# Output projection as seven block products, first gates applied earlier, second head's loads issued earlier

## The chip, the cores and the metric

The kernel runs on one core of one Trainium2 chip. The metric is device time in microseconds (us) of one execution, as the median of several runs. The engines are named as in the profile: PE (matrix products and transposes), PEld (its weight loads), DVE, ACT and POOL (elementwise work), SP (which issues most DMA transfers; its queue is written SPq, and ACT's ACTq).

## The reference, cut to what matters

One block works on x of 1024 tokens by 1024 columns in fp32:

```python
h = rms_norm(x, norm1_g[l])
z = h @ w_in[l]
glu_in, q, k, v, gate_logits = jnp.split(z, SPLITS, axis=-1)
a = a_val * jax.nn.sigmoid(a_gate)           # from glu_in
a = silu(rms_norm(causal_depthwise_conv(a, conv_w[l], conv_b[l]), conv_norm_g[l]))
y_a = a @ w_conv_out[l]
...                                          # 16 heads, three dilated windows, mixed into o
y_b = o @ w_attn_out[l]
g = jax.nn.sigmoid(gate_logits + gate_b[l])
g_a, g_b = jnp.split(g, 2, axis=-1)
x = x + (g_a * y_a + g_b * y_b) @ w_out[l]
h = rms_norm(x, norm2_g[l])
u = causal_depthwise_conv(h @ w_up[l], ffn_conv_w[l], ffn_conv_b[l])
x = x + (silu(u_gate) * u_val) @ w_down[l]
```

The change touches three things: where `sigmoid(...)` of the first half of the gates and its product with `y_a` are computed, the product with `w_out` (1024 x 1024 x 1024), and the order of some loads near the start of the attention.

## The kernel before, in words

Every fp32 operand of a product is split in two parts of the type fp32r: `hi`, a copy by ACT, and `lo`, the rest, a subtraction on DVE (`split`, L106 and L107). A product then is three matmuls, hi by hi, hi by lo and lo by hi, summed in PSUM. A full matmul takes a 128 x 128 stationary operand and 512 columns.

The program runs in stages, one after the other on PE: the products of the convolution branch and of most gates, in pairs of 128-row blocks (a stage called the pairs here); queries and keys; values; the attention; the merge; the output projection; the up and down products of the feed-forward part. Some products are already made in seven instead of eight block products (the pairs, the values, the up products). Between the heads' own matmuls the attention runs a filler (`side_steps`): the last gate products (`gate`, L138 to L140 by `gemm_half`) and the product of the convolution branch with `w_conv_out` (`conv_out`), a few steps in each of the eight slots of a head.

**Gates.** The sixteen gate blocks go unsigmoided to DRAM (`dgate`): those of the pairs from `begun` and the code around it, the last four from `gate` during the attention. `conv_out` stores y_a (`dya`).

**Merge** (`gate_pair`, `merge`). For each of eight column blocks `c` and two token halves, two gates and y_a are loaded, both gates go through the sigmoid (L1502, L1503), y_a is multiplied by the first (L1504). PE makes `yb` (24 matmuls), DVE multiplies it by the second gate (L1524), adds (L1525), and the sum is split into `mT` (L1527 on ACT, L1528 on DVE).

**Output projection** (`wo_piece`, `wo_tile`, `wo_add`). For each column half j and each of eight token tiles, `gemm_tok` runs 24 matmuls (L155 to L157) into one of the four banks of psB. The weights of a half come in four pieces of 512 KB (`raw_wo`), each split by L1535 and L1536. DVE adds the row of x (L1619), the sum goes to DRAM (`dx2`), and ACT squares it for the norm (L1621). In the second half the first half of the row is loaded back, `wo_scaled` (L1630) multiplies the row by its rstd (a power on POOL, L131) and by g2, and `transpose_raw` (L1598) turns it on PE for the up products. Beside it, `forms_ahead` prepares combinations of up weights and stores them (`dform`).

**What sets the order.** In the attention ACT, DVE, PE and POOL run in the order in which the code is written (`manual_schedule`), as ACT, DVE and PE do in the last part of the output projection and the up products. Elsewhere a planner orders the instructions. SP's order is always the planner's; `issue_after` keeps an instruction from being put ahead of another in it. SP takes its transfers one by one, in its order: one that waits for data or for a buffer holds all behind it. Each DMA of SP also waits for the one eight earlier on its semaphore.

**Attention, first heads.** Head h's queries, keys and mask are loaded by `head(h)`, its values by `values(h)`. `tiles[h + 1] = head(h + 1)` stands at place 1 of head h, with head 1's bound to the spill number `SECOND_HEAD`. `far_out`, `near_to_far` and `far_to_near` exchange the softmax statistics of the two layouts through DRAM and small DMAs (L1256, L1259, L1263); `compare` (L1267) waits for them.

Of the kernel before, what the change touches and what calls it, by code (L numbers as in the profile page):

```python
# [21 lines left out]
P = 128  # L22
D = 1024
# [32 lines left out]
BEHIND_SPILL, SECOND_HEAD = (4, 6, 9, 11), 12  # L56
GATE_PIECES = ((12, 0), (14, 2), (15, 2))
VALUE_CONVS = 3
TAIL_AT, HEAD_AT, TABLE_AT = 32, 48, 54
# [17 lines left out]
def block_kernel(ctx: ExitStack, tc: tile.TileContext, x, xT, x0, g2, pack, mask,  # L77
# [141 lines left out]

    def side_steps(hT, da, firsts, seconds):  # L220
# [43 lines left out]
        def conv_out(c, half):  # L264
            def go(w):
# [4 lines left out]
                for _ in range(KT - 1):  # L270
                    yield next(steps)
# [3 lines left out]
                sp.dma_start(dya[c][:, half * 512 : half * 512 + 512], ya)  # L275
# [59 lines left out]
    if True:  # L335
# [450 lines left out]
        def begun(n):  # L786
# [3 lines left out]
            if n < len(GLU):  # L790
                act.activation(c11[n], c11[n], AF.Sigmoid)
            else:
                sp.dma_start(dgate[PAIRS[n][0] - 16][:, 0:512], c11[n])
# [6 lines left out]
        with tc.issue_after(settled1.ins), tc.manual_schedule(engines=hand):  # L800
# [32 lines left out]
            for n, (a, b) in enumerate(PAIRS):  # L833
# [18 lines left out]
                if 0 < n <= len(GLU):  # L852
                    last_v1()
                if inner:
# [15 lines left out]
                if not glu:  # L870
                    sp.dma_start(dgate[b - 16][:, 512:1024], p5)
                if n + 1 < N:
                    sums(n + 1)
                if inner:
                    pair_first(n + 1)
                    parts(n + 1, 2, "s12")
                    odd_add()
                    conv(PULLS[2])
                    begun(n + 1)
                    conv(PULLS[3])  # L880
                else:
# [8 lines left out]
                else:  # L890
                    c21 = cst.tile([P, 512], F32, tag="f2", bufs=2, name=f"c21_{n}")
                    act.activation(c21, X, AF.Copy)
# [12 lines left out]
                else:  # L905
                    sp.dma_start(dgate[a - 16][:, 512:1024], c12)
# [136 lines left out]
        with tc.manual_schedule(engines=hand):  # L1043
# [109 lines left out]
            with tc.issue_after(spilled[-1].ins):  # L1153
                for i in range(2):
# [11 lines left out]
    if True:  # L1166
# [87 lines left out]
        def near_to_far(h):  # L1254
            for i in range(4):
# [5 lines left out]
        def far_to_near(h):  # L1261
            with tc.issue_after(queued[0].ins):
                (sp if h else act).dma_start(other[h][:, 0], dstat[h % 2].rearrange("(i a) r s -> (a r) i s", i=4))  # L1263
# [120 lines left out]
        with tc.manual_schedule(engines={ENG.Activation, ENG.DVE, ENG.PE, ENG.Pool}):  # L1384
# [9 lines left out]
            for at in range(len(slots) + BACK + 1):  # L1394
# [4 lines left out]
                if cur is not None:  # L1399
# [9 lines left out]
                    if place == 1 and h + 1 < H:  # L1409
                        with tc.issue_after(spilled[SECOND_HEAD].ins) if not h else ExitStack():  # L1410
                            tiles[h + 1] = head(h + 1)
# [52 lines left out]
                if apart(at):  # L1464
                    piece_low()
                with tc.issue_after(last_v.ins) if not at else ExitStack():
# [3 lines left out]
            for _ in gates:  # L1470
                piece_low()
                piece_high()
                o_step(heads)
    p2b_cm.__exit__(None, None, None)
    psH_cm.__exit__(None, None, None)
    psA[0] = ctx.enter_context(tc.tile_pool(name="psA2", bufs=2, space=PSUM, reuse_waits="tile"))
# [7 lines left out]
    p3_cm = tc.tile_pool(name="ph3", bufs=1, reuse_waits="tile")  # L1484
    p3 = p3_cm.__enter__()
    if True:
# [4 lines left out]
        gated = {}  # L1491

        def gate_pair(c, half):
            cs = slice(half * 512, half * 512 + 512)
            gg = p3.tile([P, 3, 512], F32, tag="e", bufs=3, name=f"gg_{c}_{half}")
# [615 lines left out]
```

## Time and profile before

| what | us |
|---|---|
| median of 3 runs (lowest, highest) | 1654.94 (1653.69, 1656.18) |
| profiled execution, device time | 1658.41 |
| its span | 1656.6 |
| PE busy in the span | 1648.5 |
| DVE busy | 1283.9 |
| ACT busy | 930.2 |
| POOL busy | 402.0 |

Stages in the profile's time: the pairs from about 70 us (the gates' among them are stored from 170.5 to 284), queries and keys to 471, values to about 560, attention to about 842, merge 843 to 930, output projection 930 to 1023, then the up and the down products.

Two kinds of rows are used below. A group row reads: line, engine, operation, tiles written and read, partitions by elements, count, then busy time and mean ns of one, then the idle time of that engine just before these instructions and what ended it. A row of the timeline or of the chain of waits starts with the time and the duration in us. The row of a window gives its bounds, its length, each engine's busy time with instruction counts (PE, PEld, DVE, ACT, POOL), the granted PE clock, the busy share of the DMA engines and GB/s.

### The profile page before, as it was taken

How to read it: one execution, taken by the hardware profiler on the slowest of the kernel's cores; microseconds unless marked ns; L12 is line 12 of the kernel's file. 1: busy time of each engine (PE TensorE's matmuls, PEld its weight loads, DVE VectorE, ACT ScalarE, POOL GpSimd, SP SyncE). 2: the span in 40 equal slices, each digit the busy share in tenths (PEclk: the TensorE clock that was granted, in tenths of full speed). 3: DMA queues.
4: the chain of work that ended last, by engine and by line, in shares of the span. 5: the costliest groups of instructions: out<-in, count | busy, mean ns of one | idle time of the engine just before them, and what ended most of it. 6: DMA issues, size and time to landing. Idle time of an engine off the chain costs nothing.

```text
span 1656.6 us, 22999 instructions
## 1 busy us (share of the span) xinstructions
PE 1648.5 (100%) x7819; PEld 1377.5 (83%) x7819; DVE 1283.9 (78%) x2032; ACT 930.2 (56%) x1762; POOL 402.0 (24%) x446
## 2 busy tenths in 40 slices
PE   9999999999999999999999999999999999999999
PEld 7888888888888888888888888888888888888887
DVE  6999988899988768777567646878767777799863
ACT  6565555788856668877655434544445444534331
POOL 0034445798830345646310000000000000000000
PEclk9999999999999999999999999999999999999999
DMA  9241235244567989978587775422222222598841
GB/s 361 84 158 52 100 116 202 89 136 127 161 202 268 354 250 279 281 226 253 154 302 250 243 292 195 153 89 89 77 89 77 79 87 89 181 387 289 284 167 51
DMA packets 183414, 303.43 MB, mean 183 GB/s; under 512 B 32128, under 2 KB 90112, under 8 KB 180992
## 3 DMA queue, kind: packets, MB, share of 16 engines
q1 hardware_dynamic: 181904, 299.20, 53.3%
q10 hardware_dynamic: 1392, 2.76, 0.4%
q8 instruction: 62, 1.02, 0.3%
q14 instruction: 56, 0.46, 0.1%
HBM read 217.36 MB, written 84.48 MB: 182 GB/s over the span
## 4 chain that ended last, share of the span: by engine, by line
PE 96%; DMA 2%; DVE 1%; ACT 1%; issue 0%; SPq 0%; DVEq 0%; ACTq 0%
PE dx L1917 7%; PE xz L163 6%; PE xz L164 6%; PE xz L165 6%; PE dy L1917 5%; PE qkv L156 3%; PE qkv L157 3%; PE qkv L155 3%; PE gx L164 3%; PE gx L165 3%; PE gx L163 3%; PE y L163 2%; PE y L164 2%; PE y L165 2%; PE pp L1291 2%; PE wo L156 2%
## 5 line engine op out<-in xcount | busy, mean ns | idle before, releaser
L594 POOL TENSOR_TENSOR codd<-codd,cpart 128x513 f32<-128x513 f32 x112 | 148.7, 1329 | 110.2 <-DVE lo_v L107 49.1
L1820 DVE SCALAR_TENSOR_TENSOR u<-u,pk 128x1023 f32<-128x1023 f32 x88 | 112.3, 1278 | 1.2 <-ACT u L1818 0.9
L155 PE MATMUL qkv<-qkv_hi,hT 128*128 128x512 f32 x256 | 102.7, 401 | 0.0
L156 PE MATMUL qkv<-qkv_lo,hT 128*128 128x512 f32 x256 | 100.2, 391 | 0.2 <-DVE qkv_lo L107 0.2
L157 PE MATMUL qkv<-qkv_hi,hT 128*128 128x512 f32 x256 | 100.3, 392 | 0.0
L643 DVE SCALAR_TENSOR_TENSOR conv<-csum,both,conv 128x512 f32<-128x512 f32 x120 | 90.2, 751 | 1.9
L643 DVE SCALAR_TENSOR_TENSOR conv<-apad,pk,conv 128x512 f32<-128x512 f32 x120 | 90.1, 751 | 1.7
L107 DVE TENSOR_TENSOR lo_uv<-raw_uv,hi_uv 128x1024 fp32r<-128x1024 f32 x20 | 24.5, 1226 | 79.2 <-ACT hi_uv L106 79.2
L608 ACT ACTIVATE cpart<-apad,pk 128x513 f32<-128x513 f32 x112 | 77.4, 758 | 11.5 <-POOL codd L594 11.4
L1313 DVE TENSOR_TENSOR pl<-pp,ph 128x512 fp32r<-128x512 f32 (+1 forms) x95 | 58.8, 619 | 29.5 <-ACT ph L1312 28.7
L1198 DVE CUSTOM_DVE_ANT_0 p<-s,m 128x512 f32<-128x512 f32 (+1 forms) x120 | 59.2, 503 | 26.0 <-POOL p L1242 15.0
L163 PE MATMUL xz<-h2left,hi_uv 128*128 128x512 f32 x176 | 68.6, 390 | 0.0
L163 PE MATMUL xz<-blk_t,hi_s3g 128*128 128x512 f32 x176 | 68.5, 389 | 0.0
L165 PE MATMUL xz<-h2left,lo_uv 128*128 128x512 f32 x176 | 68.5, 389 | 0.0
L164 PE MATMUL xz<-h2left,hi_uv 128*128 128x512 f32 x176 | 68.5, 389 | 0.0
L164 PE MATMUL xz<-blk_t,hi_s3g 128*128 128x512 f32 x176 | 68.5, 389 | 0.0
L165 PE MATMUL xz<-blk_t,lo_s3g 128*128 128x512 f32 x176 | 68.5, 389 | 0.0
L1312 ACT ACTIVATE ph<-pp 128x512 fp32r<-128x512 f32 (+1 forms) x95 | 51.3, 540 | 28.1 <-PE pp L1291 27.2
L1818 ACT ACTIVATE u<-u,pk 128x1024 f32<-128x1024 f32 x44 | 54.5, 1238 | 9.4 <-DVE u L1807 4.5
L131 POOL TENSOR_TENSOR rs<-ss,mhalf 128x8 f32<-128x8 f32 x32 | 53.7, 1679 | 23.9 <-DVE ss L130 22.8
L973 ACT ACTIVATE qn<-qkv,rs 128x64 f32<-128x64 f32 x256 | 56.4, 355 | 1.0 <-POOL rs L131 1.0
L156 PEld LDWEIGHTS qkv<-qkv_lo,hT 128*128 128x128 f32 x256 | 48.2, 188 | 10.5 <-DVE qkv_lo L107 1.0
(548 smaller groups left out, 5423.4 us busy)
## 6 DMA issues: line engine op xcount, KB each, us to landing
wr<-w_down SPq DMA_DIRECT2D x45, 512.0 KB, 5.7
kk<-dk SPq DMA_DIRECT2D x32, 512.0 KB, 6.5
gr<-dff SPq DMA_DIRECT2D x62, 256.0 KB, 5.2
raw_g<-w_ch SPq DMA_DIRECT2D x23, 512.0 KB, 3.7
dff<-u SPq DMA_DIRECT2D x22, 512.0 KB, 2.6
raw_uv<-w_up SPq DMA_DIRECT2D x21, 512.0 KB, 3.6
raw_ug<-w_up SPq DMA_DIRECT2D x20, 512.0 KB, 3.6
raw_qkv<-w_qkv SPq DMA_DIRECT2D x16, 512.0 KB, 4.9
```

Source lines behind the costliest of these rows:

```text
L155: pe.matmul(ps, ah, hi[:, k % 2, :], start=(k == 0), stop=False)
L156: pe.matmul(ps, ah, lo[:, k % 2, :], start=False, stop=False)
L157: end = pe.matmul(ps, al, hi[:, k % 2, :], start=False, stop=(k == KT - 1))
L163: pe.matmul(o, wh[:, k, :], bh[:, k, :], start=(start and k == 0), stop=False, skip_group_check=not start)
L164: pe.matmul(o, wh[:, k, :], bl[:, k, :], start=False, stop=False, skip_group_check=not start)
L165: end = pe.matmul(o, wl[:, k, :], bh[:, k, :], start=False, stop=(k == 3), skip_group_check=not start)
L594: r = pool.tensor_tensor(out=out, in0=in0, in1=in1, op=op)
L608: act.activation(part, zo[:, i : i + 513], AF.Copy, scale=taps[:, c, 2 * i + 1 : 2 * i + 2])
L643: dve.scalar_tensor_tensor(out=out_, in0=src[:, i : i + 512], scalar=w, in1=out_, op0=ALU.mult, op1=ALU.add)
L1198: dve.tensor_tensor_reduce(out=pt, in0=s, in1=m, scale=-1.0, scalar=3e38, op0=ALU.add, op1=ALU.min, accum_out=nm)
L1820: dve.scalar_tensor_tensor(out=acc[:, d:], in0=src[:, : T - d], scalar=w(2 - d), in1=acc[:, d:], op0=ALU.mult, op1=ALU.add)
L1917: pe.matmul(banks[n][:, cols], a[:, c], b[:, d], start=(start and i == 0 and m == 0), stop=(stop and i == nf - 1 and m == 2), skip_group_c ...
```

## The change

**Output projection.** The 1024 x 1024 x 1024 product is cut in 2 x 2 blocks of 512 and made from seven block products of sums, in place of eight. The token sums (`a11`, `s3`, `a12`, `a22`, `s1`, `s2`, `s4`) are formed in `merge`, which now takes the blocks in the order token half 0, c 0 to 3; half 1, c 0 to 3; half 1, c 4 to 7; half 0, c 4 to 7. The weight sums (`t1`, `t2`, `t3`, `t4`) are formed on DVE while PE works. Each block product has four token tiles of 12 matmuls (`block`): 28 blocks, 336 matmuls. The first twenty go through four banks `wa` and four `wb`, some of them summing in PSUM on top of an earlier product; the last eight (`seven`, `fourth`) stand among the transposes. Rows of x are loaded once and stay in SBUF, so the loads of `dx2` go. The combinations of up weights (`forms_ahead`) are spread over the merge and the blocks.

**First gates.** In the pairs the sigmoid of the gate blocks below 8 is taken before the store (`gate_out`, `gates_go`). During the attention `conv_out` loads the gate back (`ga`), and `times_gate` multiplies y_a by it, on POOL for 14 of the 16 halves and on DVE for two, at places 2 and 4 of a head's slots; the product is stored. The merge loses the first gate's loads, sigmoids and products.

**Loads.** Head 1's loads and the reload of hT are bound to other instructions, the statistics' small transfers are written in another order, and `far_to_near` of head 1 moves from SP's queue to ACT's.

```diff
-BEHIND_SPILL, SECOND_HEAD = (4, 6, 9, 11), 12
+BEHIND_SPILL = (4, 6, 9, 11)
+GATES_AT = (2, 4)
+FORM_AT = (6, 7, 9, 10, 11, 13, 14, 15, 16)
...
+                def times_gate():
+                    (dve if half and c > KT - 3 else pool).tensor_tensor(out=ya, in0=ya, in1=gate[0], op=ALU.mult)
+                    sp.dma_start(dya[c][:, half * 512 : half * 512 + 512], ya)
...
+        def gates_go():
+            while gates_due:
+                c, cs, t = gates_due.pop(0)
+                act.activation(t, t, AF.Sigmoid, bias=pk[:, C_GB + c : C_GB + c + 1])
+                sp.dma_start(dgate[c][:, cs], t)
...
             with tc.issue_after(spilled[-1].ins):
+                tiles[1] = head(1)
+            with tc.issue_after(queued[0].ins):
                 for i in range(2):
                     fetch(b12[i], db12[i])
...
-            for i in range(4):
+            for i in (3, 2, 0, 1):
                 queued[:] = [sp.dma_start(other[h][32 * i : 32 * i + 32, 1], own[h][:, 0, i])]
...
-                (sp if h else act).dma_start(other[h][:, 0], dstat[h % 2].rearrange("(i a) r s -> (a r) i s", i=4))
+                (sp if h > 1 else act).dma_start(other[h][:, 0], dstat[h % 2].rearrange("(i a) r s -> (a r) i s", i=4))
...
-            dve.tensor_tensor(out=ya, in0=ya, in1=ga, op=ALU.mult)
...
+            if c < 4 and not half:
+                tt_(b, ya, gb, add)
+                halves("a11", k, b)
+            elif c < 4:
+                tt_(a, ya, gb, add)
+                tt_(b, b, a, sub)
+                halves("s3", k, b)
+            elif half:
+                tt_(ya, ya, gb, add)
+                halves("a22", k, ya)
+                tt_(a, a, ya, add)
+                tt_(b, ya, b, sub)
+            else:
+                tt_(ya, ya, gb, add)
+                halves("a12", k, ya)
+                halves("s1", k, a)
+                halves("s2", k, b)
+                tt_(b, ya, b, sub)
...
+        def block(o, n, t, w, start, stop):
+            ts = slice(t % 4 * P, t % 4 * P + P)
+            th, tl = tok[n][:, 0], tok[n][:, 1]
+            for k in range(4):
+                wh, wl = (v[:, k % 2] for v in wof[w][k // 2])
+                pe.matmul(o, th[:, k, ts], wh, start=start and k == 0, stop=False, skip_group_check=not start)
+                pe.matmul(o, th[:, k, ts], wl, start=False, stop=False, skip_group_check=not start)
+                end = pe.matmul(o, tl[:, k, ts], wh, start=False, stop=stop and k == 3, skip_group_check=not start)
+            return end
...
+            for m in range(20):
+                p, t = divmod(m, 4)
+                if p == 0:
+                    block(banks_a[t], "a11", t, "b11", True, True)
+                elif p == 1:
+                    banks_b[t] = bank_ps(f"wb_{t}")
+                    block(banks_b[t], "a12", t, "b21", True, True)
+                else:
+                    block(banks_a[t], ("s2", "s1", "s4")[p - 2], t, ("t2", "t1", "b22")[p - 2], False, True)
...
+                if m == 0:
+                    for i in range(2):
+                        tt_(t1[i], b12[i], b11[i], sub)
+                if m in (1, 2):
+                    tt_(t2[m - 1], b22[m - 1], t1[m - 1], sub)
+                if m in (4, 5):
+                    w_part("t2", m - 4, t2[m - 4])
+                    s4_part(m - 4)
...
+                if m in (8, 9):
+                    w_part("t1", m - 8, t1[m - 8])
+                if m in (12, 13):
+                    w_part("b22", m - 12, b22[m - 12])
...
+                if m in FORM_AT:
+                    next(ahead, None)
```

Three places of the order show what the scheduler makes of it. First SP at the end of the values: `dv` are the stores of the values, `q`, `kk` and `m` head 1's loads, `hT` the reload for the gate products. Before:

```order
L171 DMA dv_78<-vt_4452 128x1024
L174 DMA q_4969<-dq_74 128x1024
L174 DMA kk_4970<-dk_76 64x2x1024 x2
L989 DMA m_4971<-mask 128x640
L171 DMA dv_78<-vt_4452 128x1024
L171 DMA dv_78<-qhl_2454 128x1024
L171 DMA dv_78<-qhl_2455 128x1024
L174 DMA hT_241<-db_0_80 128x2048
L174 DMA hT_242<-db_1_81 128x2048
L260 DMA dgate_100<-gs_0_5018 128x512
```

Now:

```order
L174 DMA dv_78<-vt_4464 128x1024 x2
L174 DMA dv_78<-qhl_2466 128x1024
L174 DMA dv_78<-qhl_2467 128x1024
L177 DMA q_4913<-dq_74 128x1024
L177 DMA kk_4914<-dk_76 64x2x1024 x2
L1037 DMA m_4915<-mask 128x640
L177 DMA hT_241<-db_0_80 128x2048
L177 DMA hT_242<-db_1_81 128x2048
L286 DMA ga_0_6343<-dgate_88 128x512
L270 DMA dgate_100<-gs_0_5030 128x512
```

Three stores stand ahead of head 1's four loads which stood behind them, and a gate's load stands behind hT. A few rows further, SP at the loads of head 0's values (`v`, `vf`) and of head 2's `q` and `kk`, among the small transfers of the statistics. Before:

```order
L1259 DMA dstat_144<-own_5029 128x8
L1256 DMA other_5030<-own_5029 32x4x2
L174 DMA v_5100<-dv_78 128x8x128
L1256 DMA other_5030<-own_5029 32x4x2
L174 DMA vf_5102<-dv_78 128x4x128
L174 DMA q_5104<-dq_74 128x1024
L1256 DMA other_5030<-own_5029 32x4x2 x2
L174 DMA kk_5105<-dk_76 64x2x1024 x2
```

Now:

```order
L1309 DMA dstat_144<-own_5041 128x8
L1306 DMA other_5042<-own_5041 32x4x2
L177 DMA q_5116<-dq_74 128x1024
L1306 DMA other_5042<-own_5041 32x4x2
L177 DMA kk_5117<-dk_76 64x2x1024
L1306 DMA other_5042<-own_5041 32x4x2 x2
L177 DMA v_5112<-dv_78 128x8x128
L177 DMA vf_5114<-dv_78 128x4x128
L177 DMA kk_5117<-dk_76 64x2x1024
```

Head 2's `q` and one of its two `kk` moved ahead of head 0's `v` and `vf`; the other `kk` stays behind them. Last DVE at the start of the blocks: `wsum` holds the weight sums, `lo_t` the low parts of `t2` and then of `t1`, `m_s` the low parts of `s4`, `x_0` to `x_4` the rows, `form` the combination of up weights. Now:

```order
L1540 TENSOR_TENSOR wsum<-raw_wo_1_9825,wsum 128x1024
L1540 TENSOR_TENSOR x_2_9803<-wa_9814,x_2_9803 128x512
L1540 TENSOR_TENSOR x_3_9806<-wa_9815,x_3_9806 128x512
L1540 TENSOR_TENSOR lo_t_0_9897<-wsum,hi_t_0_9896 128x1024
L110 TENSOR_TENSOR m_s_9787<-m_r_9125,m_s_9787 128x1024
L1540 TENSOR_TENSOR x_0_9797<-wb_9882,x_0_9797 128x512
L1540 TENSOR_TENSOR lo_t_1_9919<-wsum,hi_t_1_9918 128x1024
L110 TENSOR_TENSOR m_s_9787<-m_r_9125,m_s_9787 128x1024
L1540 TENSOR_TENSOR x_1_9800<-wb_9902,x_1_9800 128x512
L1540 TENSOR_TENSOR x_2_9803<-wb_9942,x_2_9803 128x512
L1540 TENSOR_TENSOR form_9939<-form_9939 128x1024
L1540 TENSOR_TENSOR x_3_9806<-wb_9959,x_3_9806 128x512
```

The low parts of `t2` stand on DVE behind the adds of the first four rows and, one by one, between those of `s4` and of the next rows.

414 lines of the change are left out of this document (273 added, 141 removed).

## The prediction

> **What bounds the kernel now.** I read the page first: the span, the busy times and the chain that ended last.
>
> ```profile
> span 1656.6 us, 22999 instructions
> PE 1648.5 (100%) x7819; PEld 1377.5 (83%) x7819; DVE 1283.9 (78%) x2032; ACT 930.2 (56%) x1762; POOL 402.0 (24%) x446
> PE 96%; DMA 2%; DVE 1%; ACT 1%; issue 0%; SPq 0%; DVEq 0%; ACTq 0%
> ```
>
> PE carries 96% of the chain. So a matmul that goes is worth its time, and work on other engines costs nothing until PE waits for it. A matmul's time is not the duration in its group's row, since matmuls overlap; it is the step from one to the next, which the chain of waits shows where PE runs without a gap, here in the down products and at a transposed tile of the output projection:
>
> ```profile
> 1571.68 5.44 PE dx L1917 x24
> ...
> 990.43 0.87 PE tq L1598 x8
> ```
>
> 5.44 / 24 = 0.2267 us for a matmul of 512 columns, 0.109 for a transpose. Next the windows: the gate products of the pairs (160 to 285), the start of the attention (560 to 600), the attention itself, the merge (840 to 928) and most of the output projection:
>
> ```profile
> 160.00:285.00 125.00, 125.00 (x554) 103.52 (x553) 108.81 (x143) 68.21 (x98) 58.63 (x46) 1.00 0.37 124
> 560.00:600.00 40.00, 36.63 (x196) 30.80 (x195) 23.96 (x98) 26.74 (x84) 18.43 (x33) 0.96 0.87 270
> 660.00:720.00 60.00, 60.00 (x374) 53.09 (x372) 45.06 (x163) 48.34 (x144) 34.82 (x58) 1.00 0.85 259
> 840.00:928.00 88.00, 87.78 (x391) 72.45 (x390) 59.21 (x79) 46.10 (x63) 0.00 (x0) 1.00 0.77 263
> 928.00:1016.00 88.00, 88.00 (x410) 73.38 (x409) 45.59 (x63) 32.75 (x54) 3.31 (x6) 1.00 0.73 262
> ```
>
> PE is full in all but 560 to 600, where 3.37 us are idle and the granted clock is 0.96. That stall is made of these rows, from the chain and from the timelines of PE, DVE and SP:
>
> ```profile
> 580.01 0.47 PE L1194 MATMUL s<-kk,q 128*128 128x512 f32 x1 [0.95 <-DMA kk<-dk]
> 585.05 1.23 SPq L1256 DMA_DIRECT2D other<-own  x2
> ...
> 588.09 0.43 SPq L1263 DMA_DIRECT2D other<-dstat  x1
> 589.97 0.67 DVE L1313 TENSOR_TENSOR pl<-pp,ph 128x512 fp32r<-128x512 f32 x1
> 594.38 0.17 DVE L1267 TENSOR_TENSOR both<-own,other 128x8 f32<-128x8 f32 x1 [3.74 <-DMA other<-dstat]
> 595.92 0.50 PE L138 MATMUL gate<-hT,hi_gt 128*128 128x512 f32 x1 [2.21 <-DVE pl L1313]
> 596.00:599.00 3.00, 3.00 (x10) 2.58 (x11) 2.17 (x9) 2.11 (x7) 2.52 (x6) 0.58 0.66 214
> 599.00:602.00 3.00, 3.00 (x17) 2.66 (x16) 0.70 (x2) 1.03 (x5) 3.00 (x5) 0.85 0.71 187
> ```
>
> Head 1's statistics are issued on SP at 588.09 and hold DVE for 3.74 us; PE waits 2.21, and then runs at a granted clock of 0.58 and 0.85 for two windows of 3 us: 3 x 0.42 + 3 x 0.15 = 1.7 us more. A late `kk` costs 0.95. Stall and slow clock together are 3.4 + 1.7 = 5.1 us; with shorter gaps, the starts of PE's instructions stand 6.4 us behind an unbroken run in 560 to 600.
>
> **Blocks: -10.9 us.** The projection is these 128 matmuls three times over:
>
> ```profile
> L156 PE MATMUL wo<-lo_wo,mT 128*128 128x512 f32 x128 | 49.7, 389 | 0.0
> ```
>
> 384 become 28 x 12 = 336, of the same shape; the 64 transposes stay. 48 x 0.2267 = 10.9 us, if the operands are ready. Rows of x stay in SBUF, so eight loads of `dx2` go, and two of `w_o` come, all off PE. The other operations of this part are priced by these groups of 830 to 1050 by a landing time in 880 to 1000, and by one of the whole span:
>
> ```profile
> L1504 DVE TENSOR_TENSOR gg<-gg 128x512 f32<-128x512 f32 x16 | 11.0, 690 | 18.0 <-DMA gg<-dya 8.3 <-ACT gg L1503 7.2 <-ACT mT L1527 1.8
> L1536 DVE TENSOR_TENSOR lo_wo<-raw_wo,hi_wo 128x1024 fp32r<-128x1024 f32 x8 | 9.8, 1222 | 7.6 <-ACT hi_wo L1535 7.2
> L1630 DVE SCALAR_TENSOR_TENSOR x<-x,s,gb 128x1024 f32<-128x1024 f32 x8 | 10.3, 1284 | 4.8 <-POOL s L131 4.8
> L1502 ACT ACTIVATE gg<-gg,pk 128x512 f32<-128x512 f32 x16 | 11.5, 721 | 22.0 <-DMA gg<-dgate 21.9
> raw_wo<-w_o SPq DMA_DIRECT2D x8, 512.0 KB, 6.4
> ...
> raw_uv<-w_up SPq DMA_DIRECT2D x21, 512.0 KB, 3.6
> ```
>
> **Merge: 0.** DVE gets 4 x (3 + 4 + 5 + 6) = 72 operations of 0.69 (the token sums and their low parts; the first gate's product is gone), 49.7 us; 8 low parts of `w_ao` and 4 of `b11` and `b21` at 1.22, 14.7; the forms of up weights, 7.1. Together 71 of the 16 x 24 x 0.2267 = 87 us in which PE makes `yb`. A block of 6 such operations (4.1) with a low part (1.2) just fits the 5.44 us of its PE work, and four PSUM banks let DVE fall some blocks behind. Uncovered, each late block would cost what DVE exceeds 5.44 by.
>
> **Waits within the blocks: +0.7.** I set t = 0 where the last `yb` ends; a block is 12 x 0.2267 = 2.72 us, twenty of them 54.4. In these DVE has 20 adds (13.8), 8 low parts of weights, 2 of `s4` and 6 weight sums at 1.22 (19.5), and the form and first scaling (about 9): 42 us or 78%, but in an order written by hand. `t2` needs `b12`, whose load waits for a raw buffer that the low part of `b21` frees: issue near 5 us, landing 4 us after it, `b22` some 6 us behind. The 4 lies between 3.6 for `raw_uv` and 6.4 for `raw_wo`, whose loads went out in bursts among the gates' that are now fewer. With two sums and the adds between, the second low part of `t2` is done near 22.7, and PE wants it in the ninth block's seventh matmul group, near 23.3. For `t1` I get 33.3 against 34.2, for `b22` 43.7 against 45.1. The margins are 0.6 to 1.4 us, less than the error of such a sum; I take 0.7 for one of them missed. What is queued behind on DVE are the adds that free the banks, so a miss also shifts the next adds, but the banks of `wa` are wanted four blocks (10.9 us) later.
>
> **Waits at the transition: +0.8.** Between the sixth transposed tile and the first product with the up sums `t2`, PE has 60 matmuls and two pairs of transposes, 13.6 + 1.7 = 15.3 us. DVE has some 12 operations of 1.22 in that stretch, 14.7, and begins about 1.5 us after PE: 0.8 late.
>
> For both I take 1.5. The lower bound is 0 (each low part in time). The upper: by `raw_wo`'s own 6.4 the loads land 2.4 later; two chains late by that, 4.8, with one slow stretch of 1.7 as after 595.92, and the 0.8: 7.3. The value is nearer the lower end, since `raw_wo` never held PE before.
>
> **Gates in the pairs: 0.** Twelve more sigmoids of 0.72 are 8.7 us of ACT, in 125 us where it is busy 68.2; four others replace copies. DVE, busy 108.8 there, gets nothing. Uncovered they would cost at most 8.7.
>
> **Gate products in the attention: 0.** Fourteen products on POOL, two on DVE (0.69 each). The nearest row for POOL with two inputs is the first here; below it are POOL's gaps in a head, and the wait of DVE for POOL in 600 to 840:
>
> ```profile
> L594 POOL TENSOR_TENSOR codd<-codd,cpart 128x513 f32<-128x513 f32 x112 | 148.7, 1329 | 110.2 <-DVE lo_v L107 49.1
> 708.82 0.37 POOL L1242 TENSOR_SCALAR p<-p,st 128x128 f32<-128x128 f32 x1 [2.55 <-DVE st L1245]
> 711.96 0.37 POOL L1242 TENSOR_SCALAR pf<-pf,both 128x128 f32<-128x128 f32 x1 [2.77 <-PE pp L1291]
> L1198 DVE CUSTOM_DVE_ANT_0 p<-s,m 128x512 f32<-128x512 f32 (+1 forms) x104 | 51.4, 504 | 21.5 <-POOL p L1242 15.0 <-PE s L1195 3.3 <-POOL far_q L1191 2.4
> ```
>
> One product is 1.33 us and a head has gaps of 2.5 us and more around these places, so it fits. Behind it stand POOL's next `p`, then the transposes of the probabilities; the filler covers a slip of a microsecond. The merge loses 16 sigmoids (11.5 us of ACT), 16 products and 4 MB of loads; PE did not wait for them, so this gives nothing.
>
> **Start of the attention: -2.4.** `far_to_near` of head 1 leaves SP, where kk, do and mask stood ahead of it, for ACT. I put its issue at 586, where the last transfers of `near_to_far` go (585.05 and 1.23 on), and by the landing time of ACT's transfer in the rows below it lands at 590.1; DVE is busy until 589.97 + 0.67 = 590.6. So the 3.74 us and with them 2.2 + 1.7 = 3.9 us of PE go. But in SP's new order head 2's `q` and one `kk` stand ahead of head 0's `v`:
>
> ```profile
> other<-dstat ACTq DMA_DIRECT2D x1, 4.0 KB, 4.1
> v<-dv SPq DMA_DIRECT2D x3, 512.0 KB, 6.1
> ...
> 570.60 1.20 SPq L174 DMA_DIRECT2D kk<-dk  x2
> ...
> 575.46 0.48 PE L1329 MATMUL o<-ph_first,v 128*128 128x512 f32 x1
> ```
>
> With the issue of `v` at 571, where `kk` was, it lands at 577.1 against its first use at 575.46: +1.5 us. The late `kk` I leave at 0.95, as its second half still stands behind. -3.9 + 1.5 = -2.4. The bounds are -6.4 (the whole of what is lost in 560 to 600) and +3 (nothing gained and `v` late by twice that).
>
> **Sum.** -10.9 - 2.4 + 1.5 = -11.8. The profiled execution of 1658.41 (span 1656.6 and 1.8 around it) becomes 1646.6; it lies 3.5 above the median of 1654.94, so the median becomes **1643.1**.
>
> [...] The rows above show a PE gap of 2.21 us, followed by windows at 0.58 and 0.85. [...] The sum takes the row.
>
> **Rivals.** (A) *DVE and the weight loads bound the blocks.* For it: margins of 0.6 to 1.4 us and a landing time of 6.4. Against: DVE is only 78% full there. With the upper bound, -10.9 - 2.4 + 7.3 = -6.0: 1648.9; it decides once the load chains slip by more than their margins.
>
> (B) *The start of the attention comes out another way.* If all waits there go and none arises in the blocks, -10.9 - 6.4 = -17.3: 1637.6. If the part does not do what it says (in SP's order head 1's loads stand behind three more stores, and `v` behind `q`), +3 and +1.5: -6.4, 1648.5.
>
> (C) *Slower: POOL's products lie on PE's path.* DVE waits for POOL's `p` already, 15.0 us over 12 heads. If POOL's sequence through a head, with 1.33 to 2.66 us more, becomes the longest chain in it, each product holds PE for its length: 14 x 1.33 = 18.6, and with the blocks' gain alone +7.7: 1662.6. It decides from the point where POOL's gaps of 2.5 us are used up. Against it: POOL is busy 34.82 of 60. There is a sign that the two engines hinder each other; one line of DVE's low parts, in the attention, has this spread:
>
> ```profile
> L205 DVE TENSOR_TENSOR lo_co<-raw_co,hi_co x16: 639/682/943, 629.9 to 777.2; 128x512 fp32r<-128x512 f32 x16
> ```
>
> The median is 682 ns and the longest 943. [...]
>
> **How the numbers follow.** The forecast 0.55, A 0.17, B with the larger gain 0.10, B with late loads 0.10, C 0.08. The range from 1637 to 1651 holds the forecast with its bounds, both B and most of A. A median within 0.2% (3.3 us, about what a measurement of this kernel can tell from no change) lies above 1651.6, in A's upper part: 0.06. Slower is C, 0.08. Faster 0.86.
>
> **What would show it.** In the changed profile: 336 matmuls of the blocks and a shorter output projection; PE full from the merge to the up products, or waits there with DVE (`lo_t`, `lo_b`) or a DMA of `w_o` as releaser (A); `both` of L1267's successor without its 3.74 us, and `o<-ph_first,v` waiting for `v` or not (B); in the attention, PE's waits and DVE's wait for POOL's `p` against 15.0 us (C). A merge in which PE waits for DVE, or a wait in the pairs, would show a term wrong that I set at 0.

## The result and the profile after

The changed kernel takes 1664.56 us (median of 6 runs, 1663.23 to 1669.04), the kernel before beside it 1655.36 (6 runs, 1653.57 to 1659.40): a ratio of 1.0060, with a 95% interval of 1.0048 to 1.0071. It is 9.2 us slower, where 11.8 us faster was forecast. The profiled execution took 1665.04 us. Its page, answering to the first rows of the prediction:

```profile
span 1663.2 us, 22953 instructions
PE 1646.8 (99%) x7771; PEld 1368.1 (82%) x7771; DVE 1327.5 (80%) x2078; ACT 938.1 (56%) x1774; POOL 420.6 (25%) x460
PE 89%; DMA 4%; DVE 3%; ACT 1%; issue 1%; POOL 0%; SPq 0%; DVEq 0%; POOLq 0%; ACTq 0%
```

PE has 48 matmuls fewer, as the change promises, and yet is on the chain for only 89% of a longer span in place of 96%: the shares of DMA (4%, before 2%) and DVE (3%, before 1%) on it have grown. The same windows as before:

```profile
160.00:285.00 125.00, 125.00 (x553) 103.52 (x552) 109.43 (x143) 75.52 (x109) 59.11 (x46) 1.00 0.37 124
560.00:600.00 40.00, 37.70 (x211) 31.56 (x210) 24.31 (x101) 27.16 (x86) 19.50 (x32) 1.00 0.95 306
660.00:720.00 60.00, 59.82 (x366) 52.09 (x365) 46.77 (x156) 46.28 (x135) 40.68 (x63) 1.00 0.90 277
840.00:928.00 88.00, 87.12 (x385) 71.38 (x384) 67.99 (x91) 43.58 (x58) 0.00 (x0) 1.00 0.79 277
928.00:1016.00 88.00, 82.19 (x359) 66.86 (x358) 63.27 (x87) 35.13 (x54) 3.68 (x5) 0.94 0.57 198
```

In the projection (928 to 1016) PE now idles 5.8 us of 88 and runs at a mean clock of 0.94. A window's busy time hides short waits and a slow clock, so I made one measure for all that follows, PE's **loss**: for each matmul or transpose the step to the next, less the step of an unbroken run (0.2266 us for 512 columns, 0.171 for 384, 0.118 for 256, 0.11 for 128), summed by stage. In us:

| kernel | to 560 | 560 to 600 | attention, 600 to 840 | merge, 840 to 940 | blocks, 940 to 1040 | up products, 1040 to 1450 | rest | all |
|---|---|---|---|---|---|---|---|---|
| before | 8.0 | 6.4 | 3.3 | 0.6 | 0.1 | 0.3 | 0.2 | 18.9 |
| changed | 7.9 | 4.1 | 5.7 | 1.8 | 10.8 | 5.8 | 0.2 | 36.3 |

The sum closes: 36.3 - 18.9 = 17.4 us of loss against 10.9 of work taken away is +6.5, and the spans differ by 1663.2 - 1656.6 = 6.6. So the gain is there, and four places give it back: the blocks (+10.7), the up products (+5.6), the attention (+2.4) and the merge (+1.2).

**The blocks.** The timeline of the changed kernel around the first blocks that need the sums `t2` (t = 0 of the prediction is at 931.5 here; columns: start, length, engine, line, operation, tiles, count, and in brackets the idle time before it and what ended it). First SP: `raw_wo` at 933.25 are both halves of b12 and the first of b22, `x` the rows, `raw_wo` at 948.22 the second half of b22:

```profile
933.25 7.25 SPq L114 DMA_DIRECT2D raw_wo<-w_o  x3
940.55 7.25 SPq L1686 DMA_DIRECT2D x<-x  x10
948.22 0.33 SPq L114 DMA_DIRECT2D raw_wo<-w_o  x1
```

Then DVE, where `wsum` at 937.18 is a sum for `t1`, the one at 954.44 the second for `t2`:

```profile
937.18 1.23 DVE L1540 TENSOR_TENSOR wsum<-raw_wo,raw_wo 128x1024 f32<-128x1024 f32 x1 [2.16 <-DMA raw_wo<-w_o]
...
946.89 0.69 DVE L1540 TENSOR_TENSOR x<-wa,x 128x512 f32<-128x512 f32 x1 [3.22 <-DMA x<-x]
...
954.44 1.23 DVE L1540 TENSOR_TENSOR wsum<-raw_wo,wsum 128x1024 f32<-128x1024 f32 x1 [5.13 <-DMA raw_wo<-w_o]
...
956.78 1.22 DVE L1540 TENSOR_TENSOR lo_t<-wsum,hi_t 128x1024 fp32r<-128x1024 f32 x1
```

PE, and behind it the window of ten us that follows (columns as in the windows above: PEclk is the third figure from the end):

```profile
958.05 0.79 PE L1719 MATMUL wa<-lo_t,m_s 128*128 128x512 f32 x1 [4.41 <-DVE lo_t L1540]
...
961.49 0.80 PE L1718 MATMUL wa<-hi_t,m_s 128*128 128x512 f32 x1 [0.94 <-ACT hi_t L1805]
...
962.75 0.79 PE L1719 MATMUL wa<-lo_t,m_s 128*128 128x512 f32 x1 [0.46 <-DVE lo_t L1540]
```

```profile
958.00:968.00 10.00, 8.55 (x18) 5.90 (x19) 7.12 (x8) 4.89 (x9) 0.00 (x0) 0.50 0.60 194
```

The last load of b22 left SP at 948.22, behind ten loads of rows. What SP itself waited for between 925 and 960 (who waits, for whom, us in total, times, longest):

```profile
SPq L114 <- DVE wsum L1540: 4.8, 1, 4.8
SPq L114 <- DVE lo_b L110: 4.2, 2, 2.8
SPq L1686 <- DMA raw_wo<-w_o: 1.7, 1, 1.7
SPq L1686 <- DMA x<-x: 0.7, 2, 0.3
SPq L114 <- DMA x<-x: 0.3, 1, 0.3
```

The second half of b12 waited for a raw buffer that the first sum for `t1` frees (937.18 + 1.23 = 938.41), and left at 938.44. Behind it seven rows left by 944.4. The last three rows and the load of b22 then each waited for the landing of the transfer eight earlier on SP, and left at 946.13, 946.81, 947.48 and 948.22, while the DMA engines were nearly full (busy share 0.91 in 940 to 950). So the 7.25 us are in good part waits for landings, and not issuing alone. With the rows behind it (first experiment) this load left at 942.73, 12.3 us after the last `yb` in place of 16.7.

DVE, whose order is written by hand, waited for it 5.13 us at the second sum, with the next adds and the low part of `t2` behind. PE waited 4.41 + 0.94 + 0.46 = 5.8 us, and the clock stood at 0.50 for ten us from 958 on: that is the rest, 4.8 us, of the 10.6 lost between 940 and 985.

**The up products.** The change does not edit them, and their last window holds 1.6 us of new idle time. The window of the kernel before, then that of the changed one, then three of PE's waits in the changed one's timeline:

```profile
1410.00:1450.00 40.00, 40.00 (x178) 33.11 (x178) 27.77 (x28) 22.26 (x27) 0.00 (x0) 1.00 0.56 190
```

```profile
1410.00:1450.00 40.00, 38.41 (x166) 30.55 (x165) 31.20 (x33) 22.54 (x27) 0.00 (x0) 1.00 0.40 134
```

```profile
1089.49 0.50 PE L166 MATMUL y<-blk_b,hi_s 128*128 128x512 f32 x1 [0.69 <-ACT p L2054]
...
1438.10 0.50 PE L168 MATMUL y<-blk_b,lo_s 128*128 128x512 f32 x1 [0.61 <-DVE lo_s L110]
...
1444.74 0.50 PE L166 MATMUL xz<-blk_t,hi_s3g 128*128 128x512 f32 x1 [0.69 <-ACT u L2052]
```

The planner had put PE's products in another sequence there. (The written order of ACT, DVE and PE ends with the first of the up products; the others, these among them, are the planner's.) Runs of matmuls by product as they start in the two traces, from 1171.6 us on:

```
before                       changed
1171.60 xz<-h2left,uv   14   1171.60 xz<-h2left,uv   24
1174.78 xz<-blk_t,s3g   12   1177.04 y<-blk_t,s       2
1177.49 xz<-h2left,uv   10   1177.50 xz<-blk_t,s     12
1179.76 y<-blk_t,s      12   1180.22 y<-blk_t,s      10
1182.48 xz<-blk_t,s3g   12   1182.48 xz<-blk_t,s3g   12
1185.20 xz<-blk_t,s     12   1185.20 y<-blk_b,s      12
```

**The attention.** POOL at one of the two places where PE falls behind, then SP and POOL at the other:

```profile
761.10 1.84 POOL L298 TENSOR_TENSOR ya<-ya,ga 128x512 f32<-128x512 f32 x1 [3.63 <-DMA ga<-dgate]
762.92 1.41 POOL L1292 TENSOR_SCALAR pf<-pf,both 128x128 f32<-128x128 f32 x4
```

```profile
688.16 0.39 SPq L299 DMA_DIRECT2D dya<-ya  x1
688.60 0.42 SPq L286 DMA_DIRECT2D ga<-dgate  x1
...
694.50 1.28 POOL L298 TENSOR_TENSOR ya<-ya,ga 128x512 f32<-128x512 f32 x1 [3.26 <-ACT ph L1362]
```

A product waits on POOL for its gate's load, and the scaling of the far probabilities, whose transposes PE wants next, stands behind it. The load goes out late because the gate's tile has one buffer: it is issued only after the product before it is done and stored. At the second place the row names a copy on ACT as what came last; the load landed within 0.02 us of that copy's end, at 694.34, and in the run below with the products on DVE the load is named there.

**The merge.** The loads of the second token half of the attention's result, first before, then now:

```profile
846.88 1.53 SPq L174 DMA_DIRECT2D oT<-do  x3
```

```profile
853.88 0.32 SPq L299 DMA_DIRECT2D dya<-ya  x1
854.29 1.61 SPq L177 DMA_DIRECT2D oT<-do  x3
```

They go out 7.4 us later, behind the last product's store.

### The profile page after: what moved, and what is told of

Same layout as the page of the kernel before. It is cut to its first block, busy times and chain, and to the rows that moved or that the text cites. A ratio compares the mean times of both kernels' runs of the same rounds, so it can differ in the third digit from the quotient of the medians.

```text
span 1663.2 us, 22953 instructions
## 1 busy us (share of the span) xinstructions
PE 1646.8 (99%) x7771; PEld 1368.1 (82%) x7771; DVE 1327.5 (80%) x2078; ACT 938.1 (56%) x1774; POOL 420.6 (25%) x460
## 4 chain that ended last, share of the span: by engine, by line
PE 89%; DMA 4%; DVE 3%; ACT 1%; issue 1%; POOL 0%; SPq 0%; DVEq 0%; POOLq 0%; ACTq 0%
PE dx L2131 7%; PE xz L166 6%; PE xz L167 6%; PE xz L168 6%; PE dy L2131 5%; PE qkv L159 3%; PE qkv L160 3%; PE qkv L158 3%; PE gx L166 3%; PE gx L167 3%; PE gx L168 3%; PE y L168 2%; PE y L166 2%; PE y L167 2%; PE pp L1341 2%; PE o L1380 1%
## 5 line engine op out<-in xcount | busy, mean ns | idle before, releaser
L2034 DVE SCALAR_TENSOR_TENSOR u<-u,pk 128x1023 f32<-128x1023 f32 (+1 forms) x88 | 110.8, 1279 | 9.4 <-ACT u L2032 9.3
L636 ACT ACTIVATE cpart<-apad,pk 128x513 f32<-128x513 f32 x112 | 77.3, 757 | 11.8 <-POOL codd L622 11.7
L166 PE MATMUL xz<-h2left,hi_uv 128*128 128x512 f32 x168 | 65.5, 390 | 0.0
L167 PE MATMUL xz<-h2left,hi_uv 128*128 128x512 f32 x168 | 65.4, 389 | 0.0
L1362 ACT ACTIVATE ph<-pp 128x512 fp32r<-128x512 f32 (+1 forms) x95 | 51.0, 537 | 22.7 <-PE pp L1341 20.9
L160 PEld LDWEIGHTS qkv<-qkv_hi,hT 128*128 128x128 f32 x256 | 48.0, 188 | 10.5
```

What stands on the lines that cost most here:

```text
L160: end = pe.matmul(ps, al, hi[:, k % 2, :], start=False, stop=(k == KT - 1))
L166: pe.matmul(o, wh[:, k, :], bh[:, k, :], start=(start and k == 0), stop=False, skip_group_check=not start)
L167: pe.matmul(o, wh[:, k, :], bl[:, k, :], start=False, stop=False, skip_group_check=not start)
L636: act.activation(part, zo[:, i : i + 513], AF.Copy, scale=taps[:, c, 2 * i + 1 : 2 * i + 2])
L2034: dve.scalar_tensor_tensor(out=acc[:, d:], in0=src[:, : T - d], scalar=w(2 - d), in1=acc[:, d:], op0=ALU.mult, op1=ALU.add)
```

## The experiments

Times are medians; a kernel's loss is by the measure above, from its one profiled execution. That loss varies where a stage is unchanged: in the attention it is 5.1 to 7.0 in the seven kernels with products on POOL at places 2 and 4, and 3.3 and 3.9 in the two without these products. The smaller steps in time have intervals that overlap that of the changed kernel; there the loss of the stage carries the reading.

**SP's order in the blocks alone.** The rows are asked for behind the loads of b22.

```diff
-        for t in range(5):
-            row(t, p3)
...
             b22 = [wo_raw(1, 1, i) for i in range(2)]
+            with tc.issue_after(staged[0].ins):
+                for t in range(5):
+                    row(t, p3)
```

> The changed kernel with one edit: on SP the ten loads of the rows x_0 to x_4 stand behind the fourth load of the second group of w_o (the second half of b22) and no longer ahead of it; PE, DVE, ACT and POOL keep their order. Theory SP (the load of b22 stood 7.3 us behind the rows, and with it the weight sum, the low part of t2 and all adds behind them on DVE): the stretch in which PE's starts fall 10.6 us behind an unbroken run goes to under 2 us, and the time falls by 9 to 11 us to about 1654. Theory DVE (the blocks' sums and low parts are simply too much for DVE in that order): at most 4 us of it go, 1661 or more.

Measured: 1661.84 us, 2.7 less than the changed kernel, ratio to before 1.0042 (1.0027 to 1.0057). The loss between 940 and 985 went from 10.6 to 7.0. The time is the one that theory DVE gave, but the rows do not show its reason: SP's order is part of the loss, and then the next wait of the same chain took over, in which DVE stands idle. DVE and PE:

```profile
948.02 0.69 DVE L1541 TENSOR_TENSOR x<-wa,x 128x512 f32<-128x512 f32 x1 [5.32 <-DMA x<-x]
...
957.39 0.51 PE L1717 MATMUL wa<-hi_t,m_s 128*128 128x512 f32 x1 [2.01 <-ACT hi_t L1807]
```

The rows now come late, and since DVE's first add stands ahead of the sums of `t2`, these wait for the rows although their own operands are there.

**The order on DVE and ACT as well.** The sums and low parts of `t2` go ahead of the adds of the first rows, and `b21`'s last low part, which frees the buffer for the next load, ahead of the sums `t1`.

```diff
+                if m == 0:
+                    with tc.issue_after(lo_b21.ins):
+                        for i in range(2):
+                            tt_(t1[i], b12[i], b11[i], sub)
+                if m in (1, 2):
+                    tt_(t2[m - 1], b22[m - 1], t1[m - 1], sub)
+                if m in (2, 3):
+                    w_part("t2", m - 2, t2[m - 2])
+                if 4 <= m < 8:
+                    add_row(m - 4, 0, banks_a[m - 4])
```

> Changed kernel with the block stage's loads and its order on DVE and ACT mended, PE's order kept: w_o's loads ahead of the rows on SP, the first halves of the rows ahead of the second; on DVE the low part of b21's second half ahead of the sums t1, the sums and low parts of t2 ahead of the adds of the first four rows; on ACT t2's high parts ahead of the squares. In the run with SP's order alone 7.0 us were left, with DVE waiting 2.2 for b12, 5.3 for x_0, and the second high part of t2 behind a square. Theory (it is a chain of waits, not DVE's load): of the 10.6 us at the blocks less than 1.5 are left, time 1664.6 - 9.5 = 1655. Theory DVE load: 5 us or more are left, 1659 or more.

Measured: 1657.67, ratio 1.0018 (1.0008 to 1.0027), 6.9 less than the changed kernel and between the times of the two theories. Its profiled execution was the longest of its ten (1663.5) and lost 7.7 us between 940 and 985, so it says where waits can arise, not what is usual. In it the wait for `t2` is down to 0.5 us, and one further along has come: DVE stands 2.2 us before a step of the up weights' form, whose buffer is still being stored (the row names no releaser; the trace has that store land at 970.76), and PE waits for an add behind it.

```profile
970.84 1.42 DVE L1541 TENSOR_TENSOR form<-form 128x512 f32<-128x512 f32 x2 [2.17 <-issue]
```

**The up products.** They were bound behind two instructions; one of them, a low part on DVE, is left out.

```diff
-            with tc.issue_after(settled.ins), tc.issue_after(formed.ins):
+            with tc.issue_after(formed.ins):
```

> Changed kernel with one edit: the up products after the first three are no longer bound behind one DVE instruction (the last low part of t4), which gives them in the planner's order the sequence of PE that the kernel before had. Theory (the planner gave the up products another order, which has waits): PE's loss between 1040 and 1450 us, 5.8 us against 0.4 before, goes to under 1.5, time 1664.6 - 4.5 = 1660. Rival (the up products suffer from loads or from DVE being late, whatever their order): within 1 us of 1664.6.

Measured: 1658.84, ratio 1.0027 (1.0018 to 1.0037), 5.7 less than the changed kernel; the loss between 1040 and 1450 fell from 5.8 to 1.5, and the window at its end is full again:

```profile
1410.00:1450.00 40.00, 39.89 (x176) 32.74 (x175) 29.31 (x29) 22.73 (x26) 0.00 (x0) 1.00 0.56 189
```

PE's order from the first up products (1032 us in the kernel before) to the end is, instruction by instruction, that of the kernel before. So the loss came from the planned order, not from the products or their loads. Why the planner chose another order (it sees that low part end later, I suppose) was not tried.

**The gates' products, on DVE.** All sixteen on DVE at the same places.

```diff
-                    (dve if half and c > KT - 3 else pool).tensor_tensor(out=ya, in0=ya, in1=gate[0], op=ALU.mult)
+                    dve.tensor_tensor(out=ya, in0=ya, in1=gate[0], op=ALU.mult)
```

> The changed kernel with all sixteen products of y_a and its gate on DVE, none on POOL, at the same places. Theory place (a product that waits for y_a stands on POOL ahead of the scaling of the far probabilities, which PE wants next): the two places near 697 and 764 us where PE falls 1.2 us behind each lose most of it, 2 us in all, 1662.5. [...]

Measured: 1665.34 (1.0068, 1.0047 to 1.0088), no gain. The loss at 760 to 780 fell from 1.5 to 0.4, that at 680 to 700 rose from 1.4 to 2.0. The row tells why, and it is not the place on POOL:

```profile
694.49 0.69 DVE L298 TENSOR_TENSOR ya<-ya,ga 128x512 f32<-128x512 f32 x1 [3.15 <-DMA ga<-dgate]
```

The wait for the gate's load moved with the product to the other engine, and now holds the scores there.

**The gates' products, later in a head.**

```diff
-GATES_AT = (2, 4)
+GATES_AT = (2, 5)
```

> Changed kernel with the products of y_a and its gate at places 2 and 5 of a head in place of 2 and 4. Theory (the product waits on POOL for its gate's load, issued behind the product before it since the gate has one buffer, and the scaling of the far probabilities waits behind it): at place 5 it stands behind that scaling, and the losses at 680 to 700 and 760 to 780, 1.4 and 1.5 us, go to 0.4 each; time 1662.5. Rival (POOL's total is what counts): the two losses stay.

Measured: 1662.69 (1.0050, 1.0035 to 1.0065), 1.9 less, and the two losses are 0.1 and 0.3. POOL near the first of the places:

```profile
692.05 1.41 POOL L1292 TENSOR_SCALAR pf<-pf,both 128x128 f32<-128x128 f32 x4 [3.10 <-DVE both L1326]
693.43 2.59 POOL L1292 TENSOR_SCALAR p<-p,both 128x512 f32<-128x512 f32 x4
696.00 1.29 POOL L298 TENSOR_TENSOR ya<-ya,ga 128x512 f32<-128x512 f32 x1
```

The same product, 1.3 us of POOL, cost nothing here when it stood behind the scaling: it was the place and the late load, not POOL's total. In the three mended kernels below, with the same places, these two losses together are 1.2 to 1.6 us, against 1.8 to 3.9 in the seven with places 2 and 4; so part of the loss can come back. All fourteen products are still on POOL, and the attention loses 0.9 us more than before the change (4.2 against 3.3): a price of 18.6 us for them, as in rival C, does not show. Single overlaps of the two engines did take longer in the changed kernel: DVE's `lo_co` took 1.76 and 1.75 us at 735.79 and 752.14 beside such a product, 0.68 in the median, and the product at 761.10 beside a `lo_co` took 1.84, 1.30 in the median.

**The last product in the merge.** It is made there with its gate loaded there, as the kernel before did with all.

```diff
+            if (c, half) == (KT - 1, 1):
+                sp.dma_start(glast, dgate[c][:, cs])
+                dve.tensor_tensor(out=ya, in0=ya, in1=glast, op=ALU.mult)
```

> Changed kernel with the last of the sixteen products made in the merge (its gate loaded there), so that the pool of the attention's tail comes free with the product before it. Theory: the loads of the second token half of the attention's result go out at about 847 in place of 854.3 us, and the loss of 1.8 us between 840 and 880 goes back to 0.6 as before; time 1663.4. Rival: the loss comes from DVE being fuller in the merge and stays.

Measured: 1661.60 (1.0039, 1.0025 to 1.0054), 3.0 less, of which the merge explains 1.4: its loss is 0.4. The loads go out at the old time:

```profile
846.40 2.24 SPq L177 DMA_DIRECT2D oT<-do  x3
```

**The gates without the blocks.** The changed program up to the end of the attention, with the projection, the merge order and the up products of before.

```diff
-            ga, gb, ya = gated[c, half] = gg[:, 0], gg[:, 1], gg[:, 2]
-            sp.dma_start(ga, dgate[c][:, cs])
+            gb, ya = gated[c, half] = gg[:, 1], gg[:, 2]
...
-            dve.tensor_tensor(out=ya, in0=ya, in1=ga, op=ALU.mult)
```

> The kernel before with the changed gates and the changed head loads, but its own output projection, merge order and up products. Theory: the start of the attention gains 2.3 us, POOL's products lose about 2.4 in the attention, the rest is as before: within 2 us of the kernel before. Rival (the gates' products or the head loads carry the loss): 4 us or more above the kernel before.

Measured: 1658.44, ratio 1.0021 (1.0011 to 1.0031): 3.8 us above the kernel before beside it, so my theory missed and the rival is nearer, though under its 4. Attention and merge lose 2.5 and 1.7 us more than before, which is about that. Moving the gates is a loss as it was done.

**The head loads.** Undone in the changed kernel, alone on the kernel before, and undone in the mended kernel below. The edit that undoes them:

```diff
             with tc.issue_after(spilled[-1].ins):
-                tiles[1] = head(1)
-            with tc.issue_after(queued[0].ins):
                 for i in range(2):
                     fetch(b12[i], db12[i])
...
-            for i in (3, 2, 0, 1):
+            for i in range(4):
...
-                (sp if h > 1 else act).dma_start(other[h][:, 0], dstat[h % 2].rearrange("(i a) r s -> (a r) i s", i=4))
+                (sp if h else act).dma_start(other[h][:, 0], dstat[h % 2].rearrange("(i a) r s -> (a r) i s", i=4))
```

> The changed kernel with the head loads, the order of the statistics' transfers and the queue of head 1's as in the kernel before. Theory (this part works as forecast): the waits at 560 to 600 us grow from 4.1 to about 6.4, 1667. Rival (it is the other parts that shortened them): no difference, 1664.6.

> The kernel before with the head loads' part of the change alone. Theory (forecast): PE's loss at 560 to 600 us goes from 6.4 to about 4, time 1652.5. Rival: the time stays within 1 us of the kernel before.

> The mended kernel with the head loads, the order of the statistics' transfers and the queue of head 1's as in the kernel before. In the changed kernel alone the same edit moved PE's loss at 560 to 600 us only from 4.1 to 4.2, where the kernel before showed 6.4. Theory (the loads as changed are worth about 2 us, as forecast): 1648.5, the loss at 560 to 600 grows by 2. Rival (that loss changes from one execution to another, and the loads' order is not what sets it): 1645.5 to 1647.5, within 1 us of the mended kernel.

Measured: 1664.74 against 1664.56 in the changed kernel; 1654.00 alone, ratio 0.9995 (0.9986 to 1.0004); 1647.22 against 1646.48 in the mended one. None shows the 2 us of the theory. With the old loads the loss at 560 to 600 was 6.4, 4.2 and 2.5 in three kernels, with the new ones 2.2 to 4.1 in eleven. With the old loads in the mended kernel, DVE's wait for head 1's statistics, 3.74 us in the profile of before and 1.99 in the changed kernel with the old loads, is:

```profile
591.78 0.17 DVE L1317 TENSOR_TENSOR both<-own,other 128x8 f32<-128x8 f32 x1 [1.58 <-DMA other<-dstat]
```

So that stall varies with the same order of loads. The profiled execution of before took 1658.41, 3.5 us over the median; a loss there 4 us longer than in the kernel with the loads alone (6.4 against 2.2) would account for it, though with one profile of each kernel this is not shown. A gain of a microsecond on average is not excluded.

**The mends together.** First the three outside the blocks, then all, with the second halves of the rows loaded later, `t1` too ahead of the adds, and the form begun two blocks later.

```diff
-FORM_AT = (6, 7, 9, 10, 11, 13, 14, 15, 16)
+FORM_AT = (6, 7, 11, 12, 13, 15, 16, 17, 18)
...
+                    with tc.issue_after(roomed.ins):
+                        for t in (4, 5, 6, 7, 0, 1, 2, 3):
+                            half_row(t, 1)
```

> The changed kernel with the three mends outside the block stage (products at places 2 and 5, last product in the merge, up products unbound); the blocks as changed. Theory (the losses add): 1664.6 - 5.4 - 2.4 - 1.4 = 1655.4, with 9 to 11 us lost at the blocks. Rival (a wait taken away comes back elsewhere): 1659 or more.

> All four mends in one kernel: products at places 2 and 5, the last product in the merge, up products unbound, and the block stage with w_o's loads ahead of the rows, t1 and t2 ahead of the adds on DVE and ACT, the second halves of the rows loaded later, and the form of up weights begun two blocks later on DVE (in the run with the sums first, DVE waited 2.2 us for a form's store and PE for an add behind it). Theory (the gain of 10.9 us is real and was eaten by waits that can each be taken away): PE's loss over the whole span 18 to 20 us, as before the change, and a time of 1643 to 1646. Rival (DVE cannot keep up in the blocks whatever the order): 5 us or more stay at the blocks, 1649 or more.

Measured: 1654.02 (0.9994, 0.9984 to 1.0003) for the three, whose blocks lose 8.0 us between 940 and 985, and **1646.48** for all (5 runs, 1646.18 to 1647.52), a ratio to the kernel before of 0.9947 (0.9935 to 0.9960): 8.5 us faster, and half a us above the theory's range. The losses added, and most of each could be taken away. Its page, its projection window, and SP in the timeline:

```profile
span 1645.3 us, 22964 instructions
PE 1637.7 (100%) x7771; PEld 1365.9 (83%) x7771; DVE 1318.8 (80%) x2078; ACT 939.9 (57%) x1774; POOL 421.2 (26%) x460
```

```profile
928.00:1016.00 88.00, 87.81 (x416) 73.02 (x416) 70.04 (x99) 39.32 (x62) 5.91 (x8) 1.00 0.69 243
```

```profile
926.12 10.88 SPq L115 DMA_DIRECT2D raw_wo<-w_o  x4
937.05 2.34 SPq L1691 DMA_DIRECT2D x<-x  x5
```

DVE is busier in that window (70.0 us) than in the changed kernel (63.3), at an almost full PE: it was not its load that held PE. All four loads of weights go first, then five half rows. The loss at 940 to 1040 is 2.2 in place of 10.8, over the whole span 18.3. What is left above the kernel before lies mainly in the blocks (2.2 against 0.1) and in the attention (4.9 against 3.3).

## Why the prediction was wrong

**Blocks, -10.9: right.** 48 matmuls went, the rest have their step; the mended kernel has 7771 instructions on PE like the changed one, and 8.5 of the 10.9 us come through.

**Waits within the blocks, +0.7: this step failed.** The prediction had the second low part of `t2` done near 22.7 us after the last `yb`; it was done at 962.7 - 931.5 = 31.2. I had `b22` leave "some 6 us behind" b12, near 11. Its second half left at 948.22, which is 16.7, and DVE had it 6.2 us later, not 4. Two waits of SP were left out of that chain: the raw buffers, which the first sums free and not the low part of `b21` alone (with the rows behind it the load still left only at 12.3), and the ten loads of rows ahead of it, the third of which had to land before it could leave. The prediction follows SP's order row by row in the attention, but not here. And DVE's order was added up as work (42 of 54 us), not followed as a chain in which an instruction that waits for a load holds all behind it (the second sum for `t2` by 5.13 us). The bound of 7.3 was too low too: it allowed one stretch of slow clock of 1.7, and the clock alone took 4.8. In place of 0.7 the term measured 10.6.

**Rival A**, "DVE and the weight loads bound the blocks", had the right place and half of the reason, at too small a price (1648.9). The loads did slip past their margins, by buffers and by their place in SP's order; DVE's load did not hold PE.

**Up products: left out.** No term and no rival spoke of them: the prediction's account ends at the transition. PE's sequence differs between the two kernels in the up products that the planner orders, and that cost 5.6 us.

**Gate products in the attention, 0: wrong by 2.4.** Rival C named the place and the engine, and priced it at 18.6 by the product's length. What cost was not the product but its wait for a load from a one-buffer tile, at two of fourteen places. That this rival's 1662.6 lies within 2 us of the measured time is luck: it put 18.6 us where 2.4 were lost. The cover that I named, gaps of 2.5 us in POOL, was used up by a wait of 3.6.

**Merge, 0: wrong by 1.2.** I counted DVE's work there, which fits. The loss came from ahead of it: with the last product at the attention's end SP's loads went out 7.4 us later, and with it in the merge at the old time. That the product held them up by keeping the buffers of the attention's end in use is my reading and not shown.

**Transition, +0.8:** in the changed kernel nothing is lost between 985 and 1020; the mended one loses 1.1 us just behind, at 1038.8, where PE waits for an add on DVE. **Gates in the pairs, 0: right:** ACT is 7.3 us busier in 160 to 285 (75.5 against 68.2), and PE stays full.

**Start of the attention, -2.4: the number met (6.4 to 4.1), the reason fell.** With the old loads the loss there was 6.4 in one profile and 4.2 and 2.5 in two others, and the runs show no gain from the new order. I had written that this execution lies 3.5 us above the median, and then took 2.4 us that were in these 3.5 off the median all the same.

**The clock:** the sum rightly took the row. Here the wait of 4.41 us was followed by ten us at 0.50. In the run with the sums first there were two waits of PE of 2.09 and 2.23 us: behind the first the clock stayed at 1.00, behind the second came three us at half speed:

```profile
967.68 0.47 PE L1721 MATMUL wa<-hi_t,m_s 128*128 128x512 f32 x1 [2.09 <-DVE x L1541]
...
972.91 0.50 PE L1721 MATMUL wa<-hi_t,m_s 128*128 128x512 f32 x1 [2.23 <-DVE x L1541]
```

```profile
964.00:970.00 6.00, 3.91 (x17) 2.92 (x17) 2.96 (x3) 2.62 (x4) 0.00 (x0) 1.00 0.96 377
...
974.00:977.00 3.00, 3.00 (x9) 2.32 (x8) 3.00 (x5) 1.29 (x2) 0.00 (x0) 0.50 0.51 187
```

## What to carry to other kernels

Where the bound engine is full, work taken off it is a gain only if every operand of the new order arrives: follow each new operand back through the queue that issues its load, in that queue's order and with what the queue itself waits for (buffers, earlier landings), and through the written order of the engine that makes it, since one waiting instruction held all behind it here (5.13 us on DVE, 4.8 on SP). Compare the order of the stages that a change does not edit as well, wherever a planner sets them. And a stall in a profiled execution that lies above the median may not be there in the median: what is earned there must not be taken off the median.

## What the runs showed of the hardware

After PE's wait of 4.41 us the granted clock stayed at 0.50 over the whole of 958 to 968, while PE was given short work with further waits of 0.94 and 0.46; the gap of 2.21 us before the change had been followed by two windows of 3 us at 0.58 and 0.85. The 5.8 us of waits thus cost 10.6. And of ten loads of 256 KB on SP's queue the first seven left within 3.9 us, 0.4 to 0.7 each; the last three and the load of 512 KB behind them left 0.67 to 0.74 us apart, each as the transfer eight earlier landed: in this program, what stands behind a burst waits for the burst's landings, not only for its issue.
